# Full attention of a hybrid encoder layer in pairs of heads, with 64-row products for the low half

## The chip, the cores and the metric

One core of a Trainium2 chip runs the whole program. The time is device microseconds (us) of one execution; the lower the better. Its engines work at the same time and wait for one another through semaphores: PE (matrix products, written to PSUM), DVE (vector), ACT (activation functions, copies), POOL (small vector work, some DMA issues), and SP (issues DMAs, among them transposing ones). In the profile PEld is PE's loading of stationary operands, SPq and DVEq are the sequencers in front of an engine, and L728 means line 728 of the kernel.

## What is computed

The reference is one encoder layer: an RMS norm, an input projection, two groups of attention heads with gates, an output projection with residual, and a final norm. The change touches group A, full attention over 1024 tokens with 8 query heads, 2 key/value heads and head dimension 64:

```python
def _gqa_blocked(q, k, v):
    ...
    def block(qi):
        sc = jnp.einsum('bqkgd,bskd->bkgqs', qi, k).astype(jnp.float32) * scale
        p = jax.nn.softmax(sc, axis=-1).astype(v.dtype)
        return jnp.einsum('bkgqs,bskd->bqkgd', p, v)
```

Here q and k are RMS-normalised per head and rotated before. Group B is a neighbourhood attention over the token grid.

## The kernel before, in words

**Precision by halves.** All products run in f16. A float32 operand is split into a high f16 half and a low half (the rest), and a product is the sum of three f16 products (high by high, high by low, low by high).

**Units and slots.** Group A is 64 units `(hh, u, h)`: key/value head hh, block u of 128 queries, query head h of four. `run_units` (L1089) makes one slot for each unit and five more (SKEW_A = 5): in slot i it calls `a_qk` for unit i, `a_lo` for unit i-1 and `a_pv` for unit i-5.
- `a_qk` (L709): PE writes the unit's 128x1024 scores to one of two PSUM tiles of the pool ps_s: two products of 512 columns (L713), in which the 128 rows hold the high and low halves of q against the high half of k twice, and two more (L715) with the low half of k twice. DVE takes the row maximum (L720) and writes a throw-away bf16 result over `hl[:, 1]`. ACT computes the exponential into p32 (float32, L722), and copies it to f16, `hl[:, 0]` (L723).
- `a_lo` (L726): DVE writes p32 minus that copy to `hl[:, 1]` (L728), and SP issues a transposing DMA of hl (L733) into pt.
- `a_pv` (L736): 24 small products of PE with pt and v (L745 to L747); after every fourth head DVE scales the sum (L751 to L754).

**Buffers.** hl and p32 of unit i lie in a ring of RING = 5 places of 4096 bytes in the store ar. With o = 4096 * (i % 5), hl takes o to o + 4096, while p32 takes o + 2048 to o + 6144:

```python
        o = 4096 * (i % RING)
        hl, p32 = carve(ar, o, [2, 1024], F16), carve(ar, o + 2048, [1024], F32)
```

The second half of p32 so lies where the next ring place has its `hl[:, 0]`.

**The order in a slot.** `Flow.step` (L118) runs, in this order: what is due in "pre", ACT's jobs, `first` (the scores with maximum and exponential, then `a_pv`), `second` (`a_lo`), what is due in "mid" (the f16 copy, among others), DVE's jobs, "post", then PE's fill, "end". PE's order is always that of the program; from unit 6 on (HAND = 6) those of DVE, ACT, POOL and SP are too, while in slots 0 to 5 a scheduler orders them.

**What fills the slots.** While group A runs, PE also works off the input projections (`proj_pair`, L482: tiles of 48 products in 8 chunks, in two PSUM buffers of the pool ps_p), about 3.7 chunks a slot. Their evacuations, the splitting of the next weights (squares L350 on ACT, scale L369 on POOL, high half L392 on ACT, low half L397 on DVE) and the rotation of q for hh = 1 are ACT's and DVE's "jobs", put into slots by a budget that counts slots, not time. The copies of B's keys (khh, L657) go over SP's queue.

**Two neighbours.** `qa_gen` (L554) splits the rotated q into the halves that are transposed to qTa: a copy on ACT (L562) and a subtraction on DVE (L563), 8 of each. `b_scores` (L796) in group B already computes scores for two heads at a time: L804 over 128 rows, then L807 over 64 rows, even head in the lower half of the array and odd head in the upper.

Of the kernel before, what the change touches and what calls it, by code (L numbers as in the profile page):

```python
# [8 lines left out]
F32 = mybir.dt.float32  # L9
F16 = mybir.dt.float16  # L10
BF16 = mybir.dt.bfloat16
AF = mybir.ActivationFunctionType
OP = mybir.AluOpType
# [3 lines left out]
P = 128  # L17
# [4 lines left out]
D = 64  # L22
# [17 lines left out]
RING, VB1 = 5, 24576  # L40
# [8 lines left out]
class Flow:  # L49
# [12 lines left out]
    def at(self, delay, pos, fn, *a):  # L62
        self.due.setdefault((self.slot + delay, pos), []).append((fn, a))
# [75 lines left out]
def kernel(ctx: ExitStack, tc: tile.TileContext, x: bass.AP, w: bass.AP, wo: bass.AP,  # L139
# [3 lines left out]
    act, dve, pool, pe, sp = nc.scalar, nc.vector, nc.gpsimd, nc.tensor, nc.sync  # L143
# [5 lines left out]
    ps_s = ctx.enter_context(tc.tile_pool(name="ps_s", bufs=2, space=PSUM))  # L149
# [4 lines left out]
    at, job = fl.at, fl.job  # L154
# [8 lines left out]
    ar = one.tile([P, 16928], F32, name="ar")  # L163
# [3 lines left out]
    def carve(store, off, shape, dt):  # L167

        n = 4 if dt == F32 else 2
        t = store[:, off // 4:off // 4 + int(np.prod(shape)) * n // 4]  # L170
        t = t if n == 4 else t.bitcast(dt)
        if len(shape) == 1:
            return t
        names = "abcdef"[:len(shape)]
        return t.rearrange(f"p ({' '.join(names)}) -> p {' '.join(names)}", **dict(zip(names, shape)))
# [6 lines left out]
    def slot(kind, shape, dt):  # L182

        off, size, n = SLOTS[kind]
        k = turn[kind] = turn.get(kind, -1) + 1
        off += k % n * size
        return area(off, shape[1:], dt) if off < AREA else carve(rq, off - AREA, shape[1:], dt)
# [4 lines left out]
    def r6(i, shape, dt, name):  # L192
        if i >= 2:
            return carve(rq, (i - 2) * 6144, shape[1:], dt)
        return one.tile(shape, dt, tag=f"r{i}", name=name)

    def tn(name, n=1, tag="t"):
        return tiny.tile([P, n], F32, tag=tag, name=name)
# [44 lines left out]
    GX, GXI, GQ, GK, SCA = 51, 52, 53, 54, 55  # L243
    SCB, NSB, FB, VF = 56, 58, 60, 62
    G2 = 70
    NSA, SHA = 80, 81

    def col(i, n=1):
        return sm[:, i:i + n]
# [203 lines left out]
    def sums_now(force=False):  # L453

        while pend and (force or "b" not in late and late.get("head", 2) == 2 and (pend[0] < 3 or fl.slot >= late.get("again", 0))):
            g = pend.pop(0)
            late["again"] = fl.slot + 2
            prep_b(g)
            try_split(g)
            if g < 3:  # L460
                at(1, "pre", prep_c, g)
                at(1, "post", prep_d, g)
                at(2, "pre", load_w, g + 2)
# [25 lines left out]
    def proj_pair(g, up, lhs, evac):  # L489

        need_w(g)
        pt = proj_tile(f"pj{g}_{up}")
        hi, lo = wp[g]
        trips = ((0, hi), (0, lo), (1, hi))
        if (g, up) in ((KVA, 0), (QA, 0)):
            seq = [(k, a, b) for a, b in ((0, hi), (1, hi), (0, lo)) for k in range(KC)]
        else:
            seq = [(k, a, b) for k in range(KC) for a, b in trips]
        for i in range(2):
            ops = [((pt[:, i], lhs(a, k, 2 * up + i), b[:, k]), dict(start=n == 0, stop=n == 23))  # L500
                   for n, (k, a, b) in enumerate(seq)]
            yield from chunks(ops, 6, (lambda: evac(pt)) if i else None)
# [4 lines left out]
    kTa = r6(0, [P, NU, 3, P], F16, "kTa")  # L507
# [5 lines left out]
    qTa = [carve(rq, 8192 * i, [NU, 4, P], F16) for i in range(2)]  # L513
    klo1 = carve(rq, 16384, [NU, P], F16)
# [39 lines left out]
    def qa_gen(hh, up):  # L554
        def evac(pt):
            g = QA + hh
            stg = slot("stg1", [P, 2, 4, P], F16)
            a, b = (0, D) if hh == 0 else (D, 0)

            def fin(q):  # L560
                d = 4 if hh else 2
                at(d, "pre", lambda: act.activation(stg[:, :, :, a:a + D], q, AF.Copy))  # L562
                at(d, "mid", lambda: dve.tensor_tensor(stg[:, :, :, b:b + D], q, stg[:, :, :, a:a + D], op=OP.subtract))  # L563

                def tr():
                    sp.dma_start_transpose(qTa[hh][:, 2 * up:2 * up + 2].rearrange("p i h t -> p (i h) t"),
                                           stg.rearrange("p i a b -> p (i a b)"))
                at(d, "post", tr)
            norm_rope(g, up, pt, 4, 0, fin)
        yield from proj_pair(QA + hh, up, from_h, evac)  # L570
# [128 lines left out]
    def group(g, gens):  # L699

        def first(gen):
            prep(g + 1)
            yield from gen
        return [first(gens[0]) if g < 16 else gens[0], *gens[1:]]


    pv, sums, pts, hls = {}, {}, {}, {}

    def a_qk(i, hh, u, h):  # L709
        s = ps_s.tile([P, 1024], F32, tag="s", name=f"s{hh}_{u}_{h}")  # L710
        q = qTa[hh][:, u, h]
        for c in range(2):
            pe.matmul(s[:, c * 512:(c + 1) * 512], q, kTa[:, 4 * c:4 * c + 4, hh], start=True, stop=False)  # L713
        for c in range(2):
            pe.matmul(s[:, c * 512:(c + 1) * 512], q, klo1[:, 4 * c:4 * c + 4] if hh else kTa[:, 4 * c:4 * c + 4, 2],  # L715
                      start=False, stop=True)
        nm = tn(f"nm{hh}_{u}_{h}")
        o = 4096 * (i % RING)
        hl, p32 = carve(ar, o, [2, 1024], F16), carve(ar, o + 2048, [1024], F32)
        dve.tensor_tensor_reduce(out=hl[:, 1].bitcast(BF16), in0=s, in1=col(SHA).to_broadcast([P, 1024]), scale=col(NSA),  # L720
                                 scalar=3e38, op0=OP.add, op1=OP.min, accum_out=nm)
        act.activation(p32, s, AF.Exp, bias=nm, scale=col(SCA))  # L722
        at(0, "mid", lambda: act.activation(hl[:, 0], p32, AF.Copy))  # L723
        hls[hh, u, h] = (hl, p32)

    def a_lo(i, hh, u, h):  # L726
        hl, p32 = hls.pop((hh, u, h))
        dve.tensor_tensor(hl[:, 1], p32, hl[:, 0], op=OP.subtract)  # L728
        if i % 4 == 3:
            pt = one.tile([P, 16, P], F16, tag="gain", name=f"pt{hh}_{u}_{h}")  # L730
        else:
            pt = carve(ar, 4096 * RING + 2048 + 4096 * (i % 4), [16, P], F16)
        sp.dma_start_transpose(pt, hl.rearrange("p a b -> p (a b)"))  # L733
        pts[hh, u, h] = pt
# [23 lines left out]
    bias = {}  # L758
# [268 lines left out]
    k, q = [kva_gen(up) for up in UP], group(1, [qa_gen(0, up) for up in UP])  # L1027
# [61 lines left out]
    def run_units(units, skew, qk, lo, pvf, n, hooks=None, by_hand=0, more=1000):  # L1089

        m, hand = len(units), ExitStack()
        for i in range(m + skew + (more < 1000)):
            back = skew + (i >= more)
            if i == by_hand:
                hand.enter_context(tc.manual_schedule(engines={e.engine for e in (act, dve, pool, sp)}))
            first = (lambda: qk(i, *units[i])) if i < m else None
            second = (lambda: lo(i - 1, *units[i - 1])) if 1 <= i <= m else None
            last = (lambda: pvf(i - back, *units[i - back])) if i >= back and i != more else None
            if qk is a_qk:
                first, last = (lambda f=first, l=last: [g() for g in (f, l) if g]), None  # L1100
            if hooks:
                hooks(i)
            fl.step(n(i), first, second, last)
            sums_now()
        return hand

    ua = [(hh, u, h) for hh in range(2) for u in range(NU) for h in range(4)]
# [6 lines left out]
    mid = (CHUNKS_A - sum(n * r for n, r in FILL_A) - FILL_A_END * SKEW_A) / (64 - n_head) + 0.02  # L1114
# [18 lines left out]
    def hooks(i):  # L1133
        if i == 0:
            late["r"] = [one.tile([P, 3072], F16, tag=f"r{j}", name=f"rest{j}") for j in range(2)]
            outer, late["inner"] = [t[:, 2048:2816].bitcast(F32) for t in late["r"]]
            make = load_bias(1, outer)
            sp.dma_start(late["inner"], headmask)
            for h in range(4):
                job("dve", 0.5, make, h, delay=h, late=0)  # L1140
        if i == 1:
            prep(13)
        if NH < i <= 2 * NH:
            at(1, "post", narrow, i - NH - 1)
        if i == 46:
            late["gout"] = one.tile([P, 1024], F32, tag="gain", name="gain_o")
            sp.dma_start(late["gout"], dap(gain_out, 0, [[0, P], [1, 1024]]))
# [9 lines left out]
    a, b = ORDER[2:4]  # L1157
# [112 lines left out]
```

## Time and profile before

| | us |
|---|---|
| three runs | 566.7, 570.4, 572.85 (median 570.4) |
| the profiled execution | 570.1 |
| its span in the trace | 568.3 |
| first to last maximum of group A (L720) | 87.3 to 345.5 |

The engines' busy time in some stretches (us of the span):

| stretch | PE | DVE | ACT | POOL |
|---|---|---|---|---|
| 87 to 115 (units 0 to 5) | 28.00 of 28.00 | 25.15 | 22.39 | 19.23 |
| 156 to 197 | 41.00 of 41.00 | 34.82 | 31.52 | 1.70 |
| 237 to 277 | 40.00 of 40.00 | 32.57 | 29.84 | 1.32 |
| 277 to 317 | 40.00 of 40.00 | 33.07 | 29.84 | 1.27 |
| 366 to 400 (group B) | 33.15 of 34.00 | 29.61 | 28.17 | 13.74 |

How to read the lines that follow: a line of a group gives line, engine, operation, result and operands by their names in the program, shapes and count, then busy us and the mean ns of one, then the engine's idle us before such instructions and what ended it. A line of the timeline gives start, length, engine, line, operation and, in brackets, the idle time before it with what ended it; some neighbours of one kind are merged (x2). A line of windows gives the stretch, its length, the busy time of each engine with the number of its instructions, the granted PE clock as a share, the DMA share and GB/s. Busy time of PE comes from modelled ends of pipelined products, so a full PE isn't a PE at its peak.

### The profile page before, as it was taken

How to read it: one execution, taken by the hardware profiler on the slowest of the kernel's cores; microseconds unless marked ns; L12 is line 12 of the kernel's file. 1: busy time of each engine (PE TensorE's matmuls, PEld its weight loads, DVE VectorE, ACT ScalarE, POOL GpSimd, SP SyncE). 2: the span in 40 equal slices, each digit the busy share in tenths (PEclk: the TensorE clock that was granted, in tenths of full speed). 3: DMA queues.
4: the chain of work that ended last, by engine and by line, in shares of the span. 5: the costliest groups of instructions: out<-in, count | busy, mean ns of one | idle time of the engine just before them, and what ended most of it. 6: DMA issues, size and time to landing. Idle time of an engine off the chain costs nothing. (4 is left out here: it accounts for less than half of the span.)

```text
span 568.3 us, 13956 instructions
## 1 busy us (share of the span) xinstructions
PE 514.6 (91%) x5583; PEld 401.5 (71%) x5583; DVE 458.2 (81%) x1018; ACT 392.0 (69%) x615; POOL 152.0 (27%) x181
## 2 busy tenths in 40 slices
PE   2678989989999999999999999999798869997994
PEld 0456877868886555578888888887686647876883
DVE  4689788989887969788699888589978978988852
ACT  5546457857969769595776867397798978875321
POOL 2395887760000000000000024333611211212210
PEclk9979999999999999999999999999999979999998
DMA  8999547889999999998999989236647999899942
GB/s 240 217 181 232 121 84 195 140 141 181 224 223 179 186 214 189 220 172 177 224 164 191 194 175 190 89 66 122 151 97 131 222 170 156 143 175 170 190 110 74
DMA packets 245539, 95.49 MB, mean 168 GB/s; under 512 B 236513, under 2 KB 237025, under 8 KB 243554
## 3 DMA queue, kind: packets, MB, share of 16 engines
q1 hardware_dynamic: 241874, 73.89, 73.0%
q0 software_dynamic: 3312, 19.92, 12.4%
q8 instruction: 43, 0.70, 0.5%
q10 hardware_dynamic: 288, 0.79, 0.5%
q14 instruction: 22, 0.18, 0.1%
HBM read 29.56 MB, written 4.19 MB: 59 GB/s over the span
## 5 line engine op out<-in xcount | busy, mean ns | idle before, releaser
L482 PE MATMUL pj<-whl,hT 128*128 128x256 f16 x2112 | 254.2, 278 | 24.3 <-DMA hT<-ar 7.3
L482 PEld LDWEIGHTS <-hT 128*128 128x128 f16 x2112 | 203.8, 99 | 61.6 <-issue 19.9
L722 ACT ACTIVATE ar<-s,nm,sm 128x1024 f32<-128x1024 f32 x64 | 76.9, 1202 | 55.1 <-DVE nm L720 53.5
L720 DVE CUSTOM_DVE_ANT_0 ar<-s,sm 128x1024 bf16<-128x1024 f32 x64 | 81.9, 1280 | 32.5 <-PE s L715 32.2
L482 PEld LDWEIGHTS <-ar 128*128 128x128 f16 x768 | 73.1, 99 | 15.5 <-issue 6.6
L728 DVE TENSOR_TENSOR ar<-ar 128x1024 f16<-128x1024 f32 x64 | 79.4, 1241 | 1.4 <-ACT ar L723 1.4
L482 PE MATMUL po<-whl,ar 128*128 128x256 f16 x576 | 69.9, 276 | 1.8 <-DVE x2b L961 1.5
L723 ACT ACTIVATE ar<-ar 128x1024 f16<-128x1024 f32 x64 | 67.6, 1057 | 2.1 <-DVE sum L752 0.3
L828 ACT ACTIVATE rq<-ar,mx,sm 128x384 f32<-128x384 f32 (+1 forms) x64 | 43.1, 673 | 28.5 <-DVE mx L827 28.3
L829 ACT ACTIVATE ar<-ar,mx,sm 128x384 f16<-128x384 f32 (+1 forms) x64 | 43.5, 680 | 2.1
L482 PE MATMUL kb<-hT,whl 128*128 128x512 f16 x192 | 44.5, 379 | 0.0
L834 DVE TENSOR_TENSOR ar<-rq,ar 128x384 f16<-128x384 f32 (+1 forms) x64 | 35.5, 554 | 8.1 <-ACT ar L829 7.9
L746 PE MATMUL pv<-va,ar 128*128 128x64 f16 x384 | 40.0, 194 | 0.0
L745 PE MATMUL pv<-va,ar 128*128 128x65 f16 x384 | 39.9, 193 | 0.0
L747 PE MATMUL pv<-va,ar 128*128 128x65 f16 x384 | 39.8, 192 | 0.0
L397 DVE SCALAR_TENSOR_TENSOR whl<-raw,sm,whl 128x512 f16<-128x512 f32 x52 | 39.5, 789 | 0.0
L745 PEld LDWEIGHTS <-ar 128*128 128x128 f16 x384 | 35.5, 96 | 5.3
L746 PEld LDWEIGHTS <-ar 128*128 128x128 f16 x384 | 35.3, 97 | 5.3
L713 PE MATMUL s<-kTa,rq 128*128 128x512 f16 x128 | 38.1, 379 | 0.0
L207 POOL DMA_DIRECT2D raw<-in_w_dram x11 | 6.7, 607 | 111.2 <-ACT ar L723 89.0
L747 PEld LDWEIGHTS <-ar 128*128 128x128 f16 x384 | 35.4, 99 | 0.0
L392 ACT ACTIVATE whl<-raw,sm 128x512 f16<-128x512 f32 x52 | 33.9, 709 | 1.4 <-POOL sm L369 1.4
(163 smaller groups left out, 918.1 us busy)
## 6 DMA issues: line engine op xcount, KB each, us to landing
raw<-in_w_dram POOLq DMA_DIRECT2D x11, 1024.0 KB, 7.5
raw<-in_wo_dram POOLq DMA_DIRECT2D x4, 1024.0 KB, 5.6
ar<-in_x_dram SPq DMA_DIRECT2D x7, 512.0 KB, 6.5
khh<-ar SPq DMA_DIRECT2D x16, 128.0 KB, 3.4
x2b<-in_x_dram POOLq DMA_DIRECT2D x4, 512.0 KB, 5.7
x<-in_x_dram POOLq DMA_DIRECT2D x4, 512.0 KB, 5.8
out_dram<-x2b SPq DMA_DIRECT2D x8, 256.0 KB, 4.9
ar<-ar SPq DMA_TRANSPOSE x112, 4.5
```

The lines of the kernel that those rows point to most:

```text
L397: dve.scalar_tensor_tensor(wp[g][1][:, q], raw[g][:, q], col(S_ + g), wp[g][0][:, q], op0=OP.mult, op1=OP.subtract)
L482: pe.matmul(*o[0], **o[1])
L713: pe.matmul(s[:, c * 512:(c + 1) * 512], q, kTa[:, 4 * c:4 * c + 4, hh], start=True, stop=False)
L720: dve.tensor_tensor_reduce(out=hl[:, 1].bitcast(BF16), in0=s, in1=col(SHA).to_broadcast([P, 1024]), scale=col(NSA), scalar=3e38, op0=OP.ad ...
L722: act.activation(p32, s, AF.Exp, bias=nm, scale=col(SCA))
L723: at(0, "mid", lambda: act.activation(hl[:, 0], p32, AF.Copy))
L728: dve.tensor_tensor(hl[:, 1], p32, hl[:, 0], op=OP.subtract)
L745: pe.matmul(o, pt[:, kt], va[:, kt, hh, v_hi], start=kt == 0, stop=False)
L746: pe.matmul(o[:, :D], pt[:, kt], va[:, kt, hh, v_lo], start=False, stop=False)
L747: pe.matmul(o, pt[:, 8 + kt], va[:, kt, hh, v_hi], start=False, stop=kt == 7)
L828: act.activation(p32, t, AF.Exp, bias=mx, scale=col(SCB + hh))
L829: act.activation(hl[:, 0], t, AF.Exp, bias=mx, scale=col(SCB + hh))
```

## The change

Group A goes by pairs of heads. In an even slot i the scores of units i and i+1 are computed into both PSUM tiles: first the four products over 128 rows, then the four low products, which now take only the high half of q (64 rows) against the low half of k, the even head in the lower half of the rows, the odd head in the upper. What is left out is the product of the two low halves. In the same slot, behind `a_pv` and `a_lo`, come both maxima, both exponentials, and the f16 copy of unit i. The odd slot has only `a_pv`, `a_lo` and the copy of unit i+1. For unit 63 `a_lo` is still called by `run_units`. `qa_gen` lays the high half of q in the half of the rows that belongs to the head's parity, so that its copy and its subtraction become two each, half as wide.

```diff
         def evac(pt):
...
-            a, b = (0, D) if hh == 0 else (D, 0)
+            s6 = stg.rearrange("p i (k e) (b d) -> p i k e b d", e=2, d=D)
...
-                at(d, "pre", lambda: act.activation(stg[:, :, :, a:a + D], q, AF.Copy))
-                at(d, "mid", lambda: dve.tensor_tensor(stg[:, :, :, b:b + D], q, stg[:, :, :, a:a + D], op=OP.subtract))
+                q5 = q.rearrange("p i (k e) d -> p i k e d", e=2)
+                for e in range(2):
+                    at(d, "pre", lambda e=e: act.activation(s6[:, :, :, e, e], q5[:, :, :, e], AF.Copy))
+                    at(d, "mid", lambda e=e: dve.tensor_tensor(s6[:, :, :, e, 1 - e], q5[:, :, :, e], s6[:, :, :, e, e], op=OP.subtract))
...
+    def a_scores(i, hh, u, hs):
+        k_lo = klo1 if hh else kTa[:, :, 2]
+        s = [ps_s.tile([P, 1024], F32, tag="s", name=f"s{hh}_{u}_{h}") for h in hs]
+        q = [qTa[hh][:, u, h] for h in hs]
+        for e in range(2):
+            for c in range(2):
+                pe.matmul(s[e][:, c * 512:(c + 1) * 512], q[e], kTa[:, 4 * c:4 * c + 4, hh], start=True, stop=False)
         for c in range(2):
-            pe.matmul(s[:, c * 512:(c + 1) * 512], q, kTa[:, 4 * c:4 * c + 4, hh], start=True, stop=False)
-        for c in range(2):
-            pe.matmul(s[:, c * 512:(c + 1) * 512], q, klo1[:, 4 * c:4 * c + 4] if hh else kTa[:, 4 * c:4 * c + 4, 2],
-                      start=False, stop=True)
...
+            for e in range(2):
+                r = slice(e * D, e * D + D)
+                pe.matmul(s[e][:, c * 512:(c + 1) * 512], q[e][r], k_lo[r, 4 * c:4 * c + 4], start=False, stop=True)
+        return s
+
+    def a_max(i, hh, u, hs, s):
+        for e, h in enumerate(hs):
+            nm = tn(f"nm{hh}_{u}_{h}")
+            o = 4096 * ((i + e) % RING)
+            hl, p32 = carve(ar, o, [2, 1024], F16), carve(ar, o + 2048, [1024], F32)
+            dve.tensor_tensor_reduce(out=hl[:, 1].bitcast(BF16), in0=s[e], in1=col(SHA).to_broadcast([P, 1024]), scale=col(NSA),
+                                     scalar=3e38, op0=OP.add, op1=OP.min, accum_out=nm)
+            hls[hh, u, h] = (hl, p32, s[e], nm)
+
+    def a_qk(i, hh, u, h, pv_of):
+        s = a_scores(i, hh, u, (h, h + 1)) if h % 2 == 0 else None
+        if pv_of:
+            pv_of()
+        if i:
+            a_lo(i - 1, *ua[i - 1])
+        if s:
+            a_max(i, hh, u, (h, h + 1), s)
+            for e in range(2):
+                hl, p32, s, nm = hls[hh, u, h + e]
+                act.activation(p32, s, AF.Exp, bias=nm, scale=col(SCA))
+        hl, p32 = hls[hh, u, h][:2]
+        act.activation(hl[:, 0], p32, AF.Copy)
...
-            second = (lambda: lo(i - 1, *units[i - 1])) if 1 <= i <= m else None
+            second = (lambda: lo(i - 1, *units[i - 1])) if 1 <= i <= m and (qk is not a_qk or i == m) else None
...
-                first, last = (lambda f=first, l=last: [g() for g in (f, l) if g]), None
+                first, last = ((lambda l=last: qk(i, *units[i], l)) if i < m else last), None
```

More of the change, by code (lines that the diff above doesn't have):

```diff
@@ L707 @@
     pv, sums, pts, hls = {}, {}, {}, {}
-    def a_qk(i, hh, u, h):
-        s = ps_s.tile([P, 1024], F32, tag="s", name=f"s{hh}_{u}_{h}")
-        q = qTa[hh][:, u, h]
-        for c in range(2):
-            pe.matmul(s[:, c * 512:(c + 1) * 512], q, kTa[:, 4 * c:4 * c + 4, hh], start=True, stop=False)
-        for c in range(2):
-            pe.matmul(s[:, c * 512:(c + 1) * 512], q, klo1[:, 4 * c:4 * c + 4] if hh else kTa[:, 4 * c:4 * c + 4, 2],
-                      start=False, stop=True)
[L717 to L724, printed above, removed]
+    def a_scores(i, hh, u, hs):
[5 more added lines that the diff above has]
+                pe.matmul(s[e][:, c * 512:(c + 1) * 512], q[e], kTa[:, 4 * c:4 * c + 4, hh], start=True, stop=False)
+        for c in range(2):
+            for e in range(2):
+                r = slice(e * D, e * D + D)
+                pe.matmul(s[e][:, c * 512:(c + 1) * 512], q[e][r], k_lo[r, 4 * c:4 * c + 4], start=False, stop=True)
+        return s
@@ L726, in a_lo @@
+    def a_qk(i, hh, u, h, pv_of):
[11 more added lines that the diff above has]
+        act.activation(hl[:, 0], p32, AF.Copy)
     def a_lo(i, hh, u, h):
-        hl, p32 = hls.pop((hh, u, h))
+        hl, p32 = hls.pop((hh, u, h))[:2]
```

## The prediction

> **What bounds the kernel now.** I read the page first (engine totals, then the costliest groups), then the busy time by windows to find the stage that the change touches, then the timeline of that stage, one engine at a time, and the list of waits.
>
> ```profile
> PE 514.6 (91%) x5583; PEld 401.5 (71%) x5583; DVE 458.2 (81%) x1018; ACT 392.0 (69%) x615; POOL 152.0 (27%) x181
> ...
> L722 ACT ACTIVATE ar<-s,nm,sm 128x1024 f32<-128x1024 f32 x64 | 76.9, 1202 | 55.1 <-DVE nm L720 53.5
> L720 DVE CUSTOM_DVE_ANT_0 ar<-s,sm 128x1024 bf16<-128x1024 f32 x64 | 81.9, 1280 | 32.5 <-PE s L715 32.2
> ...
> L728 DVE TENSOR_TENSOR ar<-ar 128x1024 f16<-128x1024 f32 x64 | 79.4, 1241 | 1.4 <-ACT ar L723 1.4
> ...
> L723 ACT ACTIVATE ar<-ar 128x1024 f16<-128x1024 f32 x64 | 67.6, 1057 | 2.1 <-DVE sum L752 0.3
> ```
>
> These are the four big vector steps of one head in full attention: the row maximum (L720), the exponential (L722), its f16 copy (L723), the f16 rest (L728, "lo"). DVE's idle time ends on PE's scores, and ACT's on DVE's maximum: both follow PE. The windows say the same of PE itself, from the maximum of unit 6 to that of unit 60:
>
> ```profile
> core 0: us, PE busy (x) PEld busy (x) DVE busy (x) ACT busy (x) POOL busy (x), PEclk, DMA share, GB/s
> 114.92:333.50 218.58, 215.85 (x2526) 158.70 (x2523) 184.76 (x325) 168.28 (x220) 18.66 (x29) 1.00 1.02 190
> ```
>
> PE is busy 215.85 of 218.58 us, at full granted clock. 54 slots take 218.58 us, 4.05 each, so **8.10 per pair of slots**. One slot, and the two rows that fix its ends:
>
> ```profile
> 114.92 1.27 DVE L720 CUSTOM_DVE_ANT_0 ar<-s,sm 128x1024 bf16<-128x1024 f32 x1
> ...
> 207.08 0.59 PE L713 MATMUL s<-kTa,rq 128*128 128x512 f16 x2
> 207.51 0.59 PE L715 MATMUL s<-kTa,rq 128*128 128x512 f16 x2
> ...
> 208.14 1.28 DVE L720 CUSTOM_DVE_ANT_0 ar<-s,sm 128x1024 bf16<-128x1024 f32 x1 [0.35 <-PE s L715]
> 209.35 1.22 DVE L728 TENSOR_TENSOR ar<-ar 128x1024 f16<-128x1024 f32 x1
> 209.47 1.20 ACT L722 ACTIVATE ar<-s,nm,sm 128x1024 f32<-128x1024 f32 x1 [1.90 <-DVE nm L720]
> 210.70 1.06 ACT L723 ACTIVATE ar<-ar 128x1024 f16<-128x1024 f32 x1
> ...
> 333.50 1.28 DVE L720 CUSTOM_DVE_ANT_0 ar<-s,sm 128x1024 bf16<-128x1024 f32 x1 [0.60 <-PE s L715]
> ```
>
> The reader should see that lo (209.35) belongs to the unit before and runs while the exponential of this one runs: DVE and ACT work side by side, one unit apart. That is what the change takes apart.
>
> **PE's part.** Two 128x512 products take 207.51 - 207.08 = 0.43 us, so a pair of heads costs 4 x 0.43 = 1.72 now. Afterwards its four low products use 64 rows each, two at a time. The second attention already does this:
>
> ```profile
> L807 PE MATMUL sb<-klo,qTb 64*128 64x256 f16 x16 | 2.3, 280 | 0.0
> ```
> ```profile
> 364.15 0.38 PE L804 MATMUL sb<-khh,qTb 128*128 128x256 f16 x2
> ...
> 367.41 0.38 PE L804 MATMUL sb<-khh,qTb 128*128 128x256 f16 x2
> 367.72 0.28 PE L807 MATMUL sb<-klo,qTb 64*128 64x256 f16 x2
> 367.94 0.72 PE L482 MATMUL pj<-whl,hT 128*128 128x256 f16 x5
> ```
>
> Two L807 together last 0.28, as long as one: they run at once. But around them PE loses time: 0.31 from the first L804 to the first L807, where two of 256 columns cost 0.215; and 0.22 from there to the next product, where two at once cost 0.11. That is about 0.10 at each change of form. A pair so costs 0.86 + 0.43 + 0.20 = 1.49: 0.23 less, 7.4 us over 32 pairs, and PE's pair would be 7.87. The Trainium skill (TensorEngine Tiling (Array Packing), Overview, Theoretical Speedup) gives up to 2x for a contraction of 64, which alone would be 0.43 a pair, 13.8 in all; the same page under Tiling Modes says that a change of mode drains the engine, and that is what the 0.10 looks like.
>
> **The new order on DVE and ACT.** In an even slot i, DVE now runs lo(i-1), max(i), max(i+1), then its jobs; in the odd slot lo(i), then its jobs. ACT runs its jobs, exp(i), exp(i+1), copy(i); then in the odd slot its jobs, copy(i+1). One more wait lies in the addresses: p32 of unit i covers bytes o+2048 to o+6144 of its ring place, and the copy of i+1 writes o+4096 to o+6144. So copy(i+1) waits until lo(i) has read p32. It had to before as well, but then lo of the unit before ran beside the exponential and ended in time (209.35 + 1.22 = 210.57, the copy starts at 210.70). Now the steps of a pair stand in one line, since copy(i) comes behind both exponentials. The handovers, from rows:
>
> ```profile
> 43.44 1.28 DVE L301 SCALAR_TENSOR_TENSOR ar<-ar,xs,gain_p 128x1024 f32<-128x1024 f32 x1
> 44.81 1.06 ACT L302 ACTIVATE ar<-ar 128x1024 f16<-128x1024 f32 x1 [0.37 <-DVE ar L301]
> ...
> 100.61 1.20 ACT L722 ACTIVATE ar<-s,nm,sm 128x1024 f32<-128x1024 f32 x1
> 101.70 0.63 ACT L562 ACTIVATE ar<-ar 128x512 f16<-128x512 f32 x1
> ...
> 213.54 1.22 DVE L728 TENSOR_TENSOR ar<-ar 128x1024 f16<-128x1024 f32 x1
> 214.68 0.68 DVE L651 SCALAR_TENSOR_TENSOR klo<-kb,ar 128x512 f16<-128x512 f32 x1
> ...
> 348.05 1.06 ACT L723 ACTIVATE ar<-ar 128x1024 f16<-128x1024 f32 x1
> ...
> 349.13 1.87 DVE L728 TENSOR_TENSOR ar<-ar 128x1024 f16<-128x1024 f32 x1 [0.56 <-ACT ar L723]
> ```
>
> Start max(i) at 0. max(i+1) starts at 1.21 (209.35 - 208.14); exp(i+1) 1.33 later (209.47 - 208.14), at 2.54; copy(i) 1.09 behind it (101.70 - 100.61), 3.63; lo(i) 1.08 later (349.13 - 348.05), 4.71; copy(i+1) 1.22 + 0.09 later (lo's length, and the 44.81 - 43.44 - 1.28 of a DVE to ACT handover), 6.02; lo(i+1) 7.10; the next maximum 1.14 behind that (214.68 - 213.54): **8.24**. That is over PE's 7.87, so the chain sets the pair. 27 pairs (units 6 to 59): 222.5 against 218.6, **+3.9**. The scores aren't on this chain: their PSUM tiles are free after exp(i+1), at 3.74, and are filled by 5.25, 3 us before the next maximum.
>
> **Jobs between.** DVE's jobs of an odd slot have only the gap from lo(i) (4.71 + 1.14 = 5.85) to lo(i+1) at 7.10, 1.25 us; in even slots 2.29 (2.42 to 4.71). ACT has 6.02 - 4.59 = 1.43 in odd slots and some 2.6 in even ones. The 27 odd slots as windows:
>
> ```profile
> 120.22:125.11 4.89, 2.32 (x22) 1.83 (x19) 4.89 (x10) 2.87 (x3) 3.48 (x3) 1.00 0.47 90
> ...
> 215.88:220.21 4.33, 4.33 (x51) 2.44 (x48) 4.33 (x6) 4.30 (x7) 0.00 (x0) 1.00 1.02 204
> ...
> 248.19:252.46 4.27, 4.27 (x60) 3.53 (x57) 4.27 (x7) 4.24 (x7) 0.00 (x0) 1.00 0.79 152
> ...
> 280.65:284.85 4.20, 4.20 (x58) 3.46 (x55) 2.43 (x3) 4.10 (x9) 0.00 (x0) 1.00 1.07 308
> ...
> sum 108.49, PE 105.92 PEld 77.49 DVE 90.80 ACT 83.00 POOL 9.48; mean PE 3.92 PEld 2.87 DVE 3.36 ACT 3.07 POOL 0.35
> ```
>
> A slot with no job has DVE busy for 2.43 (280.65), so the odd ones hold 90.80 - 27 x 2.43 = 25.2 us of jobs. The gap hides what is under 1.25: only nine exceed 2.43 + 1.25 = 3.68, the largest at 4.89, 4.33 and 4.27, by **3.9** together. Bounds: nothing, and 25.2 if no gap is used. ACT's heaviest odd slots hold three squarings or as much, and unit 8 waits for a weight's scale from POOL:
>
> ```profile
> 125.86 2.56 ACT L392 ACTIVATE whl<-raw,sm 128x512 f16<-128x512 f32 x4 [1.42 <-POOL sm L369]
> ...
> 175.53 0.61 ACT L350 ACTIVATE va<-raw 128x512 bf16<-128x512 f32 x1
> ...
> 177.65 1.19 ACT L722 ACTIVATE ar<-s,nm,sm 128x1024 f32<-128x1024 f32 x1
> ```
>
> 177.65 - 175.53 = 2.12 against 1.43, in three odd slots: **+2**. In unit 8 the four L392 end about 0.6 after the time at which exp(8) could start: +0.6. Against this, in every fifth pair the ring wraps and copy(i+1) needn't wait: 1.1 less in each of five, where jobs leave about **-2**.
>
> **Other edits.** qa_gen splits each of eight copies and subtractions in two, half as wide; same elements, one more start:
>
> ```profile
> L562 ACT ACTIVATE ar<-ar 128x512 f16<-128x512 f32 x8 | 5.0, 626 | 1.6 <-POOL ar L547 1.6
> ...
> L588 ACT ACTIVATE ar<-ar 128x256 f16<-128x256 f32 x4 | 1.6, 411 | 0.0
> ```
>
> 2 x 0.41 against 0.63 is 0.2 more each, 1.6 for eight. Four lie beside PE-led work before unit 0, four in units 4 to 8, in part in gaps: +0.5, bounds 0 and 1.6. Slots 0 to 5 are ordered by the scheduler, and DVE is nearly full in them; two maxima at once leave it less to choose from: -2 to +4, I take +1.5. The transposes on SP's queue now come two within 2.4 us, then none for 5.8. Their pt buffers are free by then; but exp(i+1) overwrites the ring place of unit i-3, whose lo ended 10.7 us before (16.48 - 8.32 + 2.54), against 11.0 now (three slots less 1.1). The wait can't be excluded behind the khh copies on the same queue: 0 to 4, I take +1. The end gives back: PE runs ahead by then. Now from max(60) at 333.50 to the first scores of the second attention at 364.15 are 30.65 us, which is 3 x 0.86 of scores and 9 slots of 3.12. Afterwards the last scores end at 5.25 and seven such slots follow: 27.1, **-3.5**.
>
> **Sum.** +3.9 + 3.9 + 2 + 0.6 - 2 + 0.5 + 1.5 + 1 - 3.5 = +7.9. The profiled execution took 570.1 us (its span 568.3), 0.3 under the median of the three runs, 570.4. Forecast **578.0**, slower.
>
> **Rivals.**
> *Faster: PE stays the bound.* If copy(i+1) didn't wait for lo(i), it would start at 4.59, lo(i+1) at 5.85, and the next maximum at 6.99: below PE's 7.87, with room for most jobs. The time would be 570.1 - 7.4 = 562.7. The point of decision is the pair's round at 7.87. For it: no row shows such a wait now. Against: the byte ranges overlap in four pairs of five. By the skill's up to 2x alone (the page named above) it would be 556.3; the same page (Performance Considerations, PSUM Bottleneck) warns that tiling doesn't speed up what empties PSUM, which speaks against this change. 12%, of which 2 for the full 2x.
> *A wash.* Jobs slide into the gaps and the ring's wrap pays in full: without 3.9 + 2 it is 572. 10%.
> *Slower still.* Projection tiles have two PSUM buffers. Afterwards a tile that PE finishes as an odd slot's filling begins (0.9 in the pair's time) is emptied among DVE's jobs of the next even slot, by 8.24 + 2.42 + 0.7 = 11.4; PE wants its buffer 2.16 slots on, at 9.5, and stands up to 1.9 us. I cost it at nothing, as the scores' 3 us of room covers it. Without that cover, some 25 tiles (3.7 chunks a slot, 8 a tile), half of them finished in odd slots, at 1 us: +12, 590. 18%.
> The forecast itself, 573 to 585, has 60%.
>
> **Numbers.** A measurement of this kernel tells about 1% (5.7 us) from no change. Faster by over 1%: two thirds of the first rival, 8%. Within 1%: its rest 4, the wash 10, a quarter of the forecast 15: 29%. Slower: 63%. The range for 8 in 10 is 566 to 592: it leaves out most of the first rival and the far end of the bounds above.
>
> **What would show it.** In the changed profile: L720 spaced 1.2 and then 7 us; the second copy of a pair starting 0.1 behind the end of L728; DVE idle before L728 on ACT's copy, some 1 to 2 us twice in a pair, and hardly any idle before L720 on PE; PE idle before the scores on ACT's exponential; the two 64-row products at once, with 0.1 lost on each side. I am wrong if PE is still busy all through with pairs under 7.9 us, or if the copy starts before lo ends.

## The result, and the profile after

The changed kernel takes **586.35 us** (median of 4 runs, 585.98 to 586.89) against 571.13 for the kernel before (566.7 to 572.85): a ratio of 1.028, with a 95% interval of 1.022 to 1.034. Here and below a ratio leaves out executions over 1.5% slower than the fastest of the same kernel, while medians are over all. It is slower, as forecast, but by 15.2 us instead of 7.9. The execution profiled took 585.98 us, with a span of 584.2; the one before had 570.1 and 568.3.

The page of the changed kernel, engine totals and costliest groups (busy us, mean ns of one, then idle us before them and what ended it). L729 is the maximum, L743 the exponential, L745 the f16 copy, L749 lo, L717 the scores over 128 rows:

```profile
PE 514.9 (88%) x5583; PEld 391.9 (67%) x5583; DVE 458.1 (78%) x1026; ACT 389.4 (67%) x623; POOL 155.9 (27%) x181
...
L749 DVE TENSOR_TENSOR ar<-ar 128x1024 f16<-128x1024 f32 x64 | 79.6, 1246 | 52.0 <-ACT ar L745 51.9
L743 ACT ACTIVATE ar<-s,nm,sm 128x1024 f32<-128x1024 f32 x64 | 76.8, 1204 | 59.3 <-DVE nm L729 52.6
...
L729 DVE CUSTOM_DVE_ANT_0 ar<-s,sm 128x1024 bf16<-128x1024 f32 x64 | 79.5, 1279 | 0.0
L745 ACT ACTIVATE ar<-ar 128x1024 f16<-128x1024 f32 x64 | 66.9, 1050 | 16.6 <-DVE ar L749 16.5
...
L717 PE MATMUL s<-kTa,rq 128*128 128x512 f16 x128 | 35.5, 382 | 12.7 <-ACT ar L743 12.7
```

Each big step takes what it took before (the means differ by at most 7 ns). What changed is who waits for whom. DVE no longer idles before the maximum (0.0, before 32.5) but before lo, on ACT's copy (52.0, before 1.4). ACT's copy waits for lo (16.6, before 2.1), and PE now waits for ACT's exponential (12.7). The windows over units 6 to 59 say it in one line (PE, PEld, DVE, ACT and POOL busy, then the granted clock); before, PE was busy for 215.85 of 218.58:

```profile
116.31:350.57 234.26, 218.01 (x2548) 151.52 (x2547) 185.04 (x328) 165.40 (x222) 20.24 (x30) 0.99 1.02 178
```

Nothing is full there any more: 16 us without PE, and DVE has 49 to spare. That is how a chain of waits looks. One plain pair, in the timelines of DVE and of ACT:

```profile
211.23 1.28 DVE L729 CUSTOM_DVE_ANT_0 ar<-s,sm 128x1024 bf16<-128x1024 f32 x1
...
212.43 1.28 DVE L729 CUSTOM_DVE_ANT_0 ar<-s,sm 128x1024 bf16<-128x1024 f32 x1
...
215.94 1.23 DVE L749 TENSOR_TENSOR ar<-ar 128x1024 f16<-128x1024 f32 x1 [0.80 <-ACT ar L745]
218.28 1.23 DVE L749 TENSOR_TENSOR ar<-ar 128x1024 f16<-128x1024 f32 x1 [1.12 <-ACT ar L745]
219.43 1.28 DVE L729 CUSTOM_DVE_ANT_0 ar<-s,sm 128x1024 bf16<-128x1024 f32 x1
```
```profile
212.55 2.41 ACT L743 ACTIVATE ar<-s,nm,sm 128x1024 f32<-128x1024 f32 x2 [2.01 <-DVE nm L729]
214.86 1.04 ACT L745 ACTIVATE ar<-ar 128x1024 f16<-128x1024 f32 x1
217.19 1.06 ACT L745 ACTIVATE ar<-ar 128x1024 f16<-128x1024 f32 x1 [1.29 <-DVE ar L749]
```

The second copy (217.19) starts as lo of the even unit ends (215.94 + 1.23 = 217.17), and the second lo as that copy ends. From maximum to maximum it is 219.43 - 211.23 = 8.20 us. This round returns to the hundredth in nine of the 27 pairs.

One pair is different. From the maximum of unit 54 at 320.41 to that of unit 56 at 334.02 the kernel takes 13.61 us. The timelines of ACT, of PE and of DMA issues (SP's and POOL's) around it:

```profile
321.73 1.20 ACT L743 ACTIVATE ar<-s,nm,sm 128x1024 f32<-128x1024 f32 x1 [2.01 <-DVE nm L729]
329.56 1.20 ACT L743 ACTIVATE ar<-s,nm,sm 128x1024 f32<-128x1024 f32 x1 [6.62 <-DMA pt<-ar]
```
```profile
330.82 1.01 PE L717 MATMUL s<-kTa,rq 128*128 128x512 f16 x2 [5.93 <-ACT ar L743]
...
340.50 1.03 PE L717 MATMUL s<-kTa,rq 128*128 128x512 f16 x4
341.46 0.60 PE L721 MATMUL s<-rq 64*128 64x512 f16 x4
342.00 0.20 PE L766 MATMUL pv<-va,ar 128*128 128x65 f16 x1
```
```profile
312.37 1.68 SPq L754 DMA_TRANSPOSE pt<-ar  x1
```
```profile
312.66 0.57 POOL L207 DMA_DIRECT2D raw<-in_w_dram  x1
```

The exponential of unit 55 overwrites the ring place of unit 51, and stood 6.62 us until the transposing DMA of unit 51, issued at 312.37, had read it. That DMA landed after 17.1 us; the longest before was 8.2 (the first line is of the changed kernel's L754, the second of the earlier kernel's L733):

```profile
DMA to landing us min/median/max: 4.2/5.4/17.1
```
```profile
DMA to landing us min/median/max: 4.2/5.0/8.2
```

At 312.66, 0.3 us after that transpose, POOL issued a weight load of 1 MB (group 11). So two things are to be told apart: the slow round of every pair, and this one stop.

| stretch, us | before | after | difference |
|---|---|---|---|
| to the maximum of unit 6 | 114.92 | 116.31 | +1.39 |
| units 6 to 59 | 218.58 | 234.26 | +15.68 |
| maximum of unit 60 to B's first scores | 30.65 | 29.40 | -1.25 |
| from there to the end of the span | 204.15 | 204.23 | +0.08 |

### The profile page after: what moved, and what is told of

The parts are those of the page before. It is cut to its first block, busy times and chain, and to the rows that moved or that the text cites. A ratio compares the mean times of both kernels' runs of the same rounds, so it can differ in the third digit from the quotient of the medians.

```text
span 584.2 us, 13937 instructions
## 1 busy us (share of the span) xinstructions
PE 514.9 (88%) x5583; PEld 391.9 (67%) x5583; DVE 458.1 (78%) x1026; ACT 389.4 (67%) x623; POOL 155.9 (27%) x181
## 5 line engine op out<-in xcount | busy, mean ns | idle before, releaser
L482 PE MATMUL pj<-whl,hT 128*128 128x256 f16 x2112 | 257.5, 280 | 26.2 <-DMA hT<-ar 8.2
L749 DVE TENSOR_TENSOR ar<-ar 128x1024 f16<-128x1024 f32 x64 | 79.6, 1246 | 52.0 <-ACT ar L745 51.9
L743 ACT ACTIVATE ar<-s,nm,sm 128x1024 f32<-128x1024 f32 x64 | 76.8, 1204 | 59.3 <-DVE nm L729 52.6
L729 DVE CUSTOM_DVE_ANT_0 ar<-s,sm 128x1024 bf16<-128x1024 f32 x64 | 79.5, 1279 | 0.0
L745 ACT ACTIVATE ar<-ar 128x1024 f16<-128x1024 f32 x64 | 66.9, 1050 | 16.6 <-DVE ar L749 16.5
L717 PE MATMUL s<-kTa,rq 128*128 128x512 f16 x128 | 35.5, 382 | 12.7 <-ACT ar L743 12.7
```

Of the source, the lines that this page charges most:

```text
L482: pe.matmul(*o[0], **o[1])
L717: pe.matmul(s[e][:, c * 512:(c + 1) * 512], q[e], kTa[:, 4 * c:4 * c + 4, hh], start=True, stop=False)
L729: dve.tensor_tensor_reduce(out=hl[:, 1].bitcast(BF16), in0=s[e], in1=col(SHA).to_broadcast([P, 1024]), scale=col(NSA), scalar=3e38, op0=OP ...
```

## The experiments

All ratios are against the kernel before in the same batch, with a 95% interval.

**Is the round a chain, with PE's saving hidden under it?** The theory on record is a chain over DVE and ACT of 8.24 us; the rival is that PE, or its PSUM tiles, still sets the pace. First, the low products go over all 128 rows again, so that PE loses its saving and all else stays:

```diff
-                pe.matmul(s[e][:, c * 512:(c + 1) * 512], q[e][r], k_lo[r, 4 * c:4 * c + 4], start=False, stop=True)
+                pe.matmul(s[e][:, c * 512:(c + 1) * 512], q[e], k_lo[:, 4 * c:4 * c + 4], start=False, stop=True)
```

> The changed kernel with the low products over all 128 rows again (the product of the two low halves comes back). PE's pair goes up by 0.23 to 8.10. If DVE and ACT set the pair at 8.20 or more, PE's loss lies in its wait for PSUM: 584 to 589 us, as the changed kernel's 586.35. If PE were the bound, 593.

Measured: 587.01 us (584.86 to 588.5), ratio 1.025 (1.021 to 1.029), beside 586.35 for the changed kernel. The pair's scores went from 1.50 to 1.73 us in its trace, and the plain round stayed at 8.20. PE's saving is worth nothing under the chain, as the theory has it. The Trainium skill (TensorEngine Tiling (Array Packing), Performance Considerations, PSUM Bottleneck) says that tiling speeds up PE but not the emptying of PSUM. The unmoved 8.20 agrees in part: the maxima and exponentials of this chain read PSUM, its copies and lo don't.

**Is it the place of the even unit's copy?** The copy of unit i goes between the two exponentials, so that lo(i) runs beside exp(i+1) and the second copy needn't wait for it:

```diff
                 act.activation(p32, s, AF.Exp, bias=nm, scale=col(SCA))
-        hl, p32 = hls[hh, u, h][:2]
-        act.activation(hl[:, 0], p32, AF.Copy)
+                if e == 0:
+                    act.activation(hl[:, 0], p32, AF.Copy)
+        else:
+            hl, p32 = hls[hh, u, h][:2]
+            act.activation(hl[:, 0], p32, AF.Copy)
```

> The changed kernel, but ACT runs the f16 copy of the even unit between the two exponentials instead of behind both. Nothing is left out. If the line of dependent steps on DVE and ACT sets the pair (8.20 us in the changed trace), it now reads: copy(i) 2.57 after the first maximum, lo(i) 3.65, copy(i+1) 4.96, lo(i+1) 6.04, next maximum 7.18. That is below PE's 7.87, so PE is the bound again: 562 to 568 us, and DVE no longer idles before lo on the copy for more than some 0.3 us. If instead the transposes, the PSUM hand-over or the two maxima in one slot as such cost the time, it stays at 580 or above.

Measured: 574.44 us (571.94 to 577.22, 10 runs), ratio 1.004 (1.001 to 1.007): 12 us faster than the changed kernel, but not 562 to 568. The timeline of DVE, then that of ACT, in this kernel (lo is L752 here, the copies L745 and L748):

```profile
142.68 1.28 DVE L729 CUSTOM_DVE_ANT_0 ar<-s,sm 128x1024 bf16<-128x1024 f32 x1
...
146.33 1.22 DVE L752 TENSOR_TENSOR ar<-ar 128x1024 f16<-128x1024 f32 x1 [0.34 <-ACT ar L745]
...
148.91 1.23 DVE L752 TENSOR_TENSOR ar<-ar 128x1024 f16<-128x1024 f32 x1
150.06 1.28 DVE L729 CUSTOM_DVE_ANT_0 ar<-s,sm 128x1024 bf16<-128x1024 f32 x1
```
```profile
145.24 1.06 ACT L745 ACTIVATE ar<-ar 128x1024 f16<-128x1024 f32 x1
146.21 1.19 ACT L743 ACTIVATE ar<-s,nm,sm 128x1024 f32<-128x1024 f32 x1
...
147.82 1.06 ACT L748 ACTIVATE ar<-ar 128x1024 f16<-128x1024 f32 x1
...
319.88 1.20 ACT L743 ACTIVATE ar<-s,nm,sm 128x1024 f32<-128x1024 f32 x1 [7.84 <-DMA pt<-ar]
```

lo(i) at 146.33 now runs beside exp(i+1) at 146.21, and the pair takes 150.06 - 142.68 = 7.38. The 24 pairs from unit 6 to 53 take 192.34 (116.09 to 308.43) against 204.10 (116.31 to 320.41). So the place of the copy is what makes the round of 8.20; but the stop is still there, 7.84 us of it at 319.88. Here too a transpose (301.15) was followed 0.3 us later by the load of group 11 (301.45).

**What is the 64-row saving worth with the old order of vector work?** Scores stay in pairs with 64-row products, while maximum, exponential and copy go back to one unit a slot:

```diff
+        if s:
+            sps[:] = s
+        a_max(i, hh, u, (h,), [sps[h % 2]])
+        hl, p32, s, nm = hls[hh, u, h]
+        act.activation(p32, s, AF.Exp, bias=nm, scale=col(SCA))
...
-        if s:
-            a_max(i, hh, u, (h, h + 1), s)
-            for e in range(2):
-                hl, p32, s, nm = hls[hh, u, h + e]
-                act.activation(p32, s, AF.Exp, bias=nm, scale=col(SCA))
-        hl, p32 = hls[hh, u, h][:2]
         act.activation(hl[:, 0], p32, AF.Copy)
```

> Only the first part of the change: the scores of two heads are computed together with 64-row low products, while maximum, exponential, copy and lo go unit by unit in the old order (lo of the unit before beside the exponential). Chain theory: no long chain, PE sets the pair at 7.87, 32 x 0.23 = 7.4 below the kernel before: 562 to 567 us. If the 64-row pairs cost more around them than they save, or if filling both PSUM tiles at once makes PE wait for the second exponential, 571 or more.

Measured: **565.09 us** (564.65 to 566.63), ratio 0.988 (0.985 to 0.991). The windows over units 6 to 59 of this kernel:

```profile
113.86:330.42 216.56, 215.48 (x2561) 152.61 (x2559) 184.79 (x328) 168.33 (x222) 18.65 (x30) 1.00 1.02 192
```

PE is full again and sets the pace. This half of the change is good; the other half, the vector steps of two heads in one slot with both copies behind both exponentials, is what costs. The gain falls short of PE's 7.4, though: to B's first scores the span gains 364.15 - 361.18 = 2.97, and behind them 2.4 more, where the code is the same. Where the rest stays was not found. That last stretch takes between 201.2 and 206.1 us in twelve of the thirteen profiled executions, for reasons that no row shows, so a us or two there can't be credited to an edit.

**Is it the weight load that makes the transposes late?** First the loads of all later groups were put two slots on:

```diff
-                at(1, "pre", load_w, g + 2)
+                at(3, "pre", load_w, g + 2)
```

> The changed kernel with the loads of the weights of the later groups issued two slots later (one number). In the changed trace one stop of about 6 us stands out at 323 to 330: the second exponential waits for a transpose that was issued beside the 1 MB weight load at 312.66, and the load itself took 15.4 us to land. If the stop comes from that meeting, it goes or moves: 579 to 582 us. If it belongs to the transposes coming in twos, or to something else at that place, the time stays at 585 to 588.

Measured: 579.68 us over four executions, one of them disturbed (1038.58); the other three took 579.19 to 579.86, ratio 1.013 (1.010 to 1.016). There was no stop, and units 6 to 59 took 228.83. That fits, but the edit moves the loads of all later groups, so it was narrowed. A delay of 2 for group 11's load alone:

```diff
-                at(1, "pre", load_w, g + 2)
+                at(2 if g == 9 else 1, "pre", load_w, g + 2)
```

> The changed kernel with only the load of weight group 11 (the one at 312.66 us) issued one slot later. If the stop at 323 to 330 comes from that load being issued in the midst of the issue of one transpose (0.3 us after its start, in three runs that show the stop), it goes: 579 to 582 us, and that load lands in under 10 us. If the stop needs only a load and transposes in twos near one another, it moves and the time stays at 584 to 588.

Measured: 587.15 us (584.73 to 589.01), ratio 1.031 (1.026 to 1.037). A miss of the edit, and a control by luck. The timeline of POOL, then the row of the transpose in SP's, in this kernel:

```profile
309.92 1.46 POOL L369 TENSOR_TENSOR sm<-wss,mh 128x1 f32<-128x1 f32 x1 [33.70 <-DVE wss L368]
311.35 0.57 POOL L207 DMA_DIRECT2D raw<-in_w_dram  x1
```
```profile
311.05 1.69 SPq L754 DMA_TRANSPOSE pt<-ar  x1
```

POOL is in order and had been waiting for the scale (L369, 33.70 us), so the later slot of the program changed nothing: the load follows the scale at 311.35, again 0.3 us behind the transpose, and the stop stayed, as the timeline of ACT shows:

```profile
329.26 1.20 ACT L743 ACTIVATE ar<-s,nm,sm 128x1024 f32<-128x1024 f32 x1 [7.64 <-DMA pt<-ar]
```

So the load was tied to something that happens later: a one-value copy on POOL from the maximum of unit 53, just ahead of the load, and in a second kernel from that of unit 55.

```diff
+        if g == 11:
+            pool.tensor_copy(raw[g][:, 0, :1], hls[ua[53]][3])
...
-                at(1, "pre", load_w, g + 2)
+                at(2 if g == 9 else 1, "pre", load_w, g + 2)
```

> The run meant to move the load of group 11 by one slot (587.15 us) left it where it was: its trace has the load at 311.35, right behind POOL's scale L369, and again 0.3 us behind the start of one transpose (311.05), with the stop behind it. Here the load also waits, by one value copied on POOL, for the maximum of unit 53, so it is issued some 2 us later, behind that transpose's issue and ahead of the next. If the stop comes from a load issued within the issue of a transpose, it goes: 578 to 582 us, and no wait of ACT on a transpose above 2 us. If any load near transposes in twos brings it, it stays: 584 to 588.

> The same with the wait on the maximum of unit 55, two slots on: the load is issued some 10 us later, behind the transposes of units 52 and 53. Both theories of the stop expect it to go if it needs that one meeting: 578 to 582 us. If loads bring a stop wherever they stand among transposes in twos, it moves and the time stays at 584 to 588; if the weights then come late for their squares, the time goes up by a few us more.

Measured: **577.69 us** (576.25 to 578.37, 10 runs), ratio 1.006 (1.004 to 1.008), with the load at 315.46; and 580.37 (578.44 to 582.02), ratio 1.011 (1.006 to 1.016), with the load at 323.56 and a delay of 4 in place of 2. The transposes landed within 9.1 us in both. The first kernel's ACT at the place of the stop, in the timeline, and the windows of units 6 to 59:

```profile
321.89 2.41 ACT L745 ACTIVATE ar<-s,nm,sm 128x1024 f32<-128x1024 f32 x2 [2.01 <-DVE nm L731]
324.20 1.99 ACT L747 ACTIVATE ar<-ar 128x1024 f16<-128x1024 f32 x2
```
```profile
116.44:344.11 227.67, 218.37 (x2587) 153.47 (x2586) 185.02 (x328) 165.51 (x222) 20.50 (x31) 1.00 1.00 183
```

The two exponentials stand back to back, and the pair takes 6.99 instead of 13.61 (the ring wraps there, so the copies, too, run without a wait). From unit 6 on, all other pairs are as in the changed kernel to 0.01 us. The one load, 2.8 us later, was worth 7.0 us in the rows: 6.6 in units 6 to 59 and 0.4 up to B's first scores. The medians differ by 8.7 for this kernel and by 6.0 for the second; behind B's first scores the two gained 1.6 and 0.4, which no row explains. The kernel before was slower in this batch, too (574.16 against 571.13), so these sizes are good to some 3 us; that the stop goes with the load's place is not in doubt.

**Do the two causes add?** With both edits, the copy between and the late loads of the first kind:

> The copy between the exponentials (as in the run with 574.44 us) and the later groups' weight loads two slots later together. That run's trace still had one stop of 7.8 us on a transpose beside the load at 301.45. If the shorter line of steps and the stop are two separate causes, their gains add: 574.4 - 6.7 = 567 to 569 us, with a mean pair of about 8.0. If the stop only moves, or the shorter line of steps brings new waits for transposes, 572 or more.

Measured: 575.61 us, with a spread of 569.31 to 588.81 over 10 runs, ratio 1.004 (1.000 to 1.008). The ratio leaves out four executions of 580.56 and more. A miss. The profiled execution is the slowest of the ten: there another load came 0.4 us behind a transpose (164.71 and 164.31) and landed after 21.2 us, so the move of all loads had only moved the meeting. What the faster executions did isn't shown. The same move on the kernel with the old order of vector work:

> Scores in pairs with the old order of the vector work (565.09 us), and the later loads two slots later. That kernel's trace has no such stop, so the later loads should bring nothing: 563 to 567 us. If loads cost by being near transposes at all, a few us less; if they come too late for the squares of the weights, more than 567.

Measured: 573.57 us (571.54 to 575.94), ratio 1.006 (1.003 to 1.009), a miss as well: later loads alone cost 8.5 us there (565.09 without). In the traces 3.1 of it lie before unit 6, 1.5 in units 6 to 59 and 4.4 behind B's first scores; the cause stays open. So the right test is the one load:

> The copy between the exponentials (574.44 us, with one stop of 7.8 us behind the load at 301.45) with only that load held until the maximum of unit 53, as in the run with 577.69 us. If the line of steps and the stop are two separate causes, their gains add: 565 to 568 us. That the run with all later loads moved two slots gave 575.61 instead would then be the price of moving the other loads (the same edit cost the kernel with only the scores in pairs 8.5 us). If the shorter line itself runs into the transposes, 572 or more.

Measured: **564.53 us** (563.71 to 565.45), ratio 0.986 (0.979 to 0.994), a little under the range expected: the two add up, and the kernel beats the one before. It ends level with the 565.09 above. Its windows from 116 to 332, nearly all of units 6 to 59:

```profile
116.00:332.00 216.00, 213.23 (x2556) 150.40 (x2554) 186.97 (x326) 164.94 (x222) 19.91 (x30) 1.00 1.08 193
```

PE is busy for 213.23 of 216.00 us: with the chain at 7.2 to 7.4 in its plain pairs (198.57 to 205.76 is one of 7.19), PE is the bound again. One wait of 2.6 us on a transpose is left (174.87).

**Can the second copy be freed in another way?** It wrote beside the ring place, so that no address stood against it, with the late loads of the first kind:

```diff
-        act.activation(hl[:, 0], p32, AF.Copy)
+        act.activation(aside(i) if h % 2 else hl[:, 0], p32, AF.Copy)
...
+        src = carve(ar, 4096 * ((i - 1) % RING), [2, 1024], F16) if h % 2 else hl
+        sp.dma_start_transpose(pt, src.rearrange("p a b -> p (a b)"))
```

> The changed kernel with the later loads moved (579.68 us), and the odd unit's f16 copy written to the second half of the next ring place, where it doesn't overlap p32 of the even unit; both copies stay behind both exponentials. Left out: the odd heads' weights aren't transposed, the even head's are transposed twice. If the overlap in the ring makes copy(i+1) wait for lo(i), the wait goes: copy(i+1) at 4.6, lo(i+1) at 5.85, next maximum at 7.0 plus what the odd slot's jobs add (25.2 us over 27 slots, 0.9 each): pairs near 7.9, where PE sets them, 566 to 573 us. If the overlap costs nothing, 578 to 581.

Measured: 589.92 us (587.03 to 592.9), ratio 1.035 (1.029 to 1.041), a miss. Its timeline of DVE, then a row of ACT's:

```profile
213.44 1.28 DVE L729 CUSTOM_DVE_ANT_0 ar<-s,sm 128x1024 bf16<-128x1024 f32 x1
...
218.16 2.36 DVE L752 TENSOR_TENSOR ar<-ar 128x1024 f16<-128x1024 f32 x2 [0.80 <-ACT ar L745]
220.66 1.28 DVE L729 CUSTOM_DVE_ANT_0 ar<-s,sm 128x1024 bf16<-128x1024 f32 x1
```
```profile
223.08 1.21 ACT L743 ACTIVATE ar<-s,nm,sm 128x1024 f32<-128x1024 f32 x1 [3.52 <-DMA pt<-ar]
```

Where nothing disturbs it, the pair does what the address theory says: both lo back to back, 7.22 from 213.44 to 220.66, near the 6.99 of the prediction's rival. But the edit holds the even ring place until a second transpose has read it, and exponentials wait for that (3.52 at 223.08). The sum says nothing about the wait it removed; the single pair does.

## Why the prediction was right, and where it was short

The measured 586.35 lies in the range of 566 to 592, but above the 573 to 585 that the prediction gave to its own mechanism. The mechanism was right; that the range also held the stop, which was not foreseen at this size, is luck.

**The chain.** Right, to 0.04 us: 8.20 for a plain pair against 8.24. Each handover that it listed is there: maxima 1.20 apart and then 7.00; the second copy 0.02 behind the end of lo (0.1 was said); DVE idle for 0.80 and 1.12 before the two lo (1 to 2 was said, a little much). That it is the copy's place which makes the chain is shown by the kernel with the copy between the exponentials, and that lo's reading holds the second copy by the 7.22 of the last experiment and the 6.99 of the pair where the ring wraps.

**PE's part.** Right: 1.50 from 340.50 to 342.00 against 1.49, with 0.10 lost before the 64-row products (0.96 for the first four, where 0.86 is due) and 0.11 behind them (0.54 where 0.43 is due). The Trainium skill's rule that a change of mode drains the engine (TensorEngine Tiling (Array Packing), Tiling Modes) agrees with these rows. That the saving is hidden was also right.

**Jobs and wrap.** The kernel without the stop is the fair test, as its 27 pairs hold nothing else: 27 x 8.20 = 221.4, longer pairs +8.82, shorter ones -2.55, together 227.67. The prediction had 222.5, +6.5 for jobs and unit 8, and -2 for the wrap: 227.0. The single sizes are off by 2.3 at most, and the sum is right to 0.7. The start (+1.39) fits the +1.5 for the first slots, but this says little: kernels with the same code up to there reached unit 6 between 115.03 and 116.44.

**The transposes: the step that failed.** The prediction put +1 us, bounds 0 and 4, on "exp(i+1) overwrites the ring place of unit i-3". It had the right instruction, the right place in the ring and the right queue. It compared how long before each the lo had ended (10.7 and 11.0 us), and so took the transpose's own time as unchanged. It named SP's queue alone; the weight load on POOL's queue was not followed, though the change moves it against the transposes, from 2.0 us ahead of one to 0.3 behind. In the earlier kernel's timelines of POOL and SP:

```profile
301.63 0.57 POOL L207 DMA_DIRECT2D raw<-in_w_dram  x1
```
```profile
303.64 3.93 SPq L733 DMA_TRANSPOSE pt<-ar  x1
```

The stop is 6.62 us of wait, past the upper bound, and taking the meeting away is worth 7.0 in the rows and 6.0 to 8.7 in the medians. Without it the changed kernel takes 577.69; the forecast was 578.0. So close a match is in part luck. Against the kernel before in its batch the kernel without the stop is 3.5 us slower (577.69 and 574.16), where 7.9 was said. In the profiled executions it is 7.4 slower, but with 1.6 us gained behind B's first scores, where nothing was forecast.

**The end.** -3.5 was said, -1.25 came. The prediction let PE run ahead of the chain, so that the last scores end 5.25 us after the maximum of unit 60. After the stop PE was no longer ahead. The timeline of PE in the changed kernel:

```profile
357.20 0.61 PE L721 MATMUL s<-rq 64*128 64x512 f16 x4
357.74 0.20 PE L766 MATMUL pv<-va,ar 128*128 128x65 f16 x1
...
379.97 0.38 PE L825 MATMUL sb<-khh,qTb 128*128 128x256 f16 x2
```

They end at 357.74, 7.17 after 350.57, and the seven slots that follow take 22.23, 3.18 each (3.12 was said). Without the stop they did end after 5.13 us, but then PE stood 1.5 us on a projection tile's evacuation, the seven slots took 23.88, and the gain was 1.6. So of the missing 2.3 us, 1.9 stands in the rows as PE's lost lead, but with the lead back only 0.4 came in.

**The rivals.** "PE stays the bound" fell as a forecast, but its mechanism is the cure: with the copy freed and the stop away the time is 564.53, where it said 562.7. "A wash" fell by its mechanism: the jobs didn't slide into the gaps but made pairs longer, by 8.82 in all; in time alone, the kernel without the stop (ratio 1.006) is not far from it. "PE stands on projection tiles" has little support: it needed 12 us, PE's waits before them come to 4.3 in units 6 to 59 of the changed kernel, and the sum closes without it.

## What to carry to other kernels

When two steps of a software pipeline are put into one slot, write down the round of dependent steps over all engines, with the byte ranges of shared buffers, before counting what an engine saves: the saving counts only where that round is shorter than the bound engine's work. Here it mattered which of two independent steps came first on an in-order engine, 1 us of copy before 1.2 us of exponential or behind it. And when a change shifts the timing of a stage, follow every DMA that is in flight with the ones on the chain, on all queues, and don't take the landing times of the old kernel as a bound: the longest of these transposes took 8.2 us there, and 17.1 after the shift.

## What the runs showed that was not expected

A transposing DMA and a 1 MB load issued by POOL 0.3 us behind it made each other late, in four kernels: transposes of up to 17.1 us in the changed kernel, 18.6 with the copy between and 18.1 in the control, with waits of 6.6 to 7.8 us behind them in each. With the load 2.0 us ahead of a transpose, or 2.9 or 11.1 behind the one that it had met, the longest landing was 8.2 to 9.1. But a load close behind a transpose isn't enough. In the kernel with the second copy aside, the timelines of SP and of POOL have the same order 0.25 us apart, and the transpose landed after 9.1 us, the load after 7.0, with no wait behind them:

```profile
285.20 6.36 SPq L758 DMA_TRANSPOSE pt<-ar  x1
```
```profile
285.45 0.57 POOL L207 DMA_DIRECT2D raw<-in_w_dram  x1
```

In the kernel before, a load 0.19 us behind a transpose of B's q (160.39 and 160.20) landed after 6.2. What else must come together was not found. The DMA queues of the changed kernel in a usual stretch (296 to 308) and in the stop (316 to 328), packets, MB and share of the engines' time; q1 carries the transposes:

```profile
q1 hardware_dynamic: 7315, 1.84, 89.7%
```
```profile
q1 hardware_dynamic: 1490, 0.37, 72.4%
q0 software_dynamic: 144, 1.05, 49.5%
```

In the stop a fifth of q1's packets take 72% of the engines' time, where 90% was enough for all. What inside the DMA engines does this stays open: no run here shows more than the two issues and the effect of moving one of them.

After PE had stood for 5.93 us, its granted clock was half for a while. The windows of the changed kernel:

```profile
325.00:330.00 5.00, 0.00 (x0) 0.00 (x0) 0.00 (x0) 0.44 (x1) 0.00 (x0) 0.96 1.33 96
330.00:335.00 5.00, 4.18 (x35) 2.26 (x35) 3.26 (x3) 4.97 (x7) 0.00 (x0) 0.50 1.23 171
```

Without the stop the clock is 1.00 in both stretches. The Trainium skill (TensorE: Matmul & The Clock Gate, Part 1: The HAM clock gate) says that about 3.4 us of idleness halves the clock; the 0.50 agrees. It cost the chain nothing, as the next pair takes 8.31 with and without it. What it took from PE may be part of the lead of 1.9 us that was missing at the end; no run separates the two.
